# A block inverse in a streaming encoder layer: the first products of its last doubling step get their PSUM bank from a turning pair

## The chip, the core and the metric

The kernel runs on one core of a Trainium2 chip. The metric is the device time of one execution in microseconds (us), lower is better. One execution is also recorded by the hardware profiler; its rows name the engines PE (matrix products), PEld (loading of weights into PE), DVE (vector engine), ACT (scalar engine), POOL (GpSimd) and SP (which issues most transfers).

## What is computed

One layer of an encoder (depth 1) for 512 prompt tokens and 64 sample tokens of width 1024, all in float32. The first half of the layer mixes tokens in two ways from one input projection: four heads of a gated delta rule (GDN), and four heads of differential attention. Then come attention to a memory of 256 tokens and a feed-forward network of width 4096. The change lies in the delta rule, which the reference writes so:

```python
a_sys = jnp.where(strict, bc[..., :, None] * kk * gam, 0.0) + jnp.eye(C)
u = triangular_solve(a_sys, bc[..., None] * vc, lower=True, unit_diagonal=True)
w = triangular_solve(a_sys, (bc * jnp.exp(G))[..., None] * kc, ...)
def step(S, xs):                      # over chunks
    vn = u_c - w_c @ S
    o = qg_c @ S + qk_c @ vn
    S = S * gl_c + kd_c.T @ vn
```

So each chunk of tokens needs a triangular system solved, and the state S passes from chunk to chunk.

## The kernel before, in words

The kernel cuts the 512 prompt tokens into four chunks of 128 (0 to 3) and treats the sample as a fifth (4), with two heads packed into each block. `gdn_prep` (line 653) makes what a chunk needs without the state: normed keys and queries, decay factors, the key products `At`, and the transposed inverse `X` of the unit triangular matrix. The inverse starts from blocks of 2 and doubles: five levels in the loop of line 757 reach blocks of 64. In each level PE turns a block (`bt`) and makes one product (`by`), ACT copies the turned block (line 765), DVE masks the product (766), PE makes the second product (767), and DVE subtracts it (773, 774). A last step from 64 to 128 stands in lines 776 to 788, for chunks 0 to 3 alone: the turned inverse is copied to `X` (line 776), four small products are written to `by` (781) and copied to `Y` (782), and four more give the corner of `X` (785 to 788).

`gdn_scan` (line 814) takes the state through a chunk: it subtracts the state's part from the values (line 830), applies `X` and scales (831 to 833, `vn`), forms the output (840), forms the state's increment in a bank (841) and updates the state `S` on DVE (line 797), and later turns the normed output (850). The sample's scan is cut into steps that lie among the attention heads.

PSUM has eight banks of 512 float32 columns, which line 75 deals out by tag: three to projections (`pr`), two that turn (`ba`), one each to even and odd chunks (`g0`, `g1`), one to the scans (`gs`). `bank(tag)` (line 100) asks for the next bank of a tag; with one bank per tag the next user waits until the last reader is done, with two they take turns. The memory's turned tiles (`turn_memory`, line 905) and the state's increment (line 841) also ask for `ba`. The key tile `kd` of a chunk (line 679) is one of two that take turns between chunks, and it is read last by the chunk's state increment.

The main loop (914 to 924) asks in this order: `gdn_prep` of chunk 0, then for c from 0 to 3 `gdn_prep` of chunk c+1, after c = 0 the memory's turned tiles and the projection `z`, the finish of the scan before, and `gdn_scan` of chunk c. Behind it `diff_project` and `diff_head` (965, 1075) are called for the four attention heads. The program is not run in that order: a scheduler lays out each engine's instructions beforehand, so products of the projections (`pr`, lines 173 to 189) for heads 0 and 1 are laid among the small products of the delta rule. Each engine runs its own row in order.

Of the kernel before, what the change touches and what calls it, by code (L numbers as in the profile page):

```python
# [37 lines left out]
def hybrid_layer_kernel(  # L38
# [40 lines left out]
    def nm(s):  # L79
        uid[0] += 1  # L80
        return f"{s}_{uid[0]}"
# [18 lines left out]
    def bank(tag="ba"):  # L100
        return ps.tile([P, 512], F32, tag=tag, name=nm(tag), bufs=BANKS[tag])
# [4 lines left out]
    def mm(out, lhsT, rhs, start=True, stop=True, pin=False, skip_group_check=False):  # L106
        i = nc.tensor.matmul(out, lhsT, rhs, start=start, stop=stop, skip_group_check=skip_group_check)  # L107
        if pin:
            tc.keep_in_program_order(i)
# [543 lines left out]
    def gdn_prep(c, nb, L):  # L653
# [91 lines left out]
        def pairs(b, half, f):  # L745
            t = b[:, 256 * half : 256 * half + np_ * P].rearrange("p (i n) -> p i n", n=P)
            for i in range(np_):
                f(t[:, i, :], i)
            return t
# [7 lines left out]
        while lv <= last:  # L757
# [6 lines left out]
            by = pairs(b, 0, lambda o, i: mm(o, As[:, i, :], low[:, i * n : (i + 1) * n]))  # L764
# [11 lines left out]
        A.copy(X, each(tr, of(Dt)))  # L776
        if lv < size:
            G.memset(Y[:64, :, :64], 0.0)
            by = bank(f"g{c % 2}")
            for h in range(H):  # L780
                mm(by[64:, h * 64 : h * 64 + 64], At[:, h, 64:], Dt[:, h, :64])
            A.copy(Y[64:, :, :64], by[64:, :256].rearrange("p (h n) -> p h n", h=4))
            bx = bank(f"g{c % 2}")
            for h in range(H):
                mm(bx[:64, h * 64 : h * 64 + 64], Y[:, h, :64], X[:, h, 64:])
            V.tensor_scalar(
                X[:64, :, 64:], bx[:64, :256].rearrange("p (h n) -> p h n", h=4), -1.0, None, ALU.mult
            )
# [124 lines left out]

    S, behind = None, lambda: None
    prepared = [gdn_prep(*chunks[0])]
    for c, _, L in chunks[:4]:
        prepared.append(gdn_prep(*chunks[c + 1]))
        if c == 0:
            turn_memory()
            project_z()  # L920
        behind()
        S, behind = gdn_scan(c, L, prepared[c], S)
        if c == 3:
            behind()
# [792 lines left out]
```

## Time and profile before

| what | value |
|---|---|
| time, median of 3 runs | 977.6 us (976.36 to 977.66) |
| the profiled execution's own time | 977.09 us |
| its span, first to last instruction | 975.3 us |
| PE busy | 960.4 us, 98% of the span, 6399 instructions |
| PEld busy | 889.9 us, 91% |
| DVE busy | 689.4 us, 71% |
| ACT busy | 536.9 us, 55% |
| bytes moved | 96.01 MB, mean 98 GB/s |

The profile's busy time of PE runs from the start of a product to its modelled end; products overlap, so a row of four that starts 0.45 us before the next row can be shown as 0.61 us long. Durations of steps are therefore taken here from start to start. A float32 product of 128x128 stands twice in the trace for each time that the program's order names it (x4 in the order is x8 in the trace); a turn stands once.

### The profile page before, as it was taken

To read this page: it belongs to the slowest core of one execution; us is meant where nothing else is said; L and a number is where in the kernel's file an instruction comes from. 1 tells how busy PE (TensorE), PEld (TensorE's weight loads), DVE (VectorE), ACT (ScalarE), POOL (GpSimd) and SP (SyncE) were. 2 spreads that over 40 slices of the span, in tenths; PEclk is the share of its full clock that TensorE was granted. 3 is DMA by queue.
4 is the path that set the end of the run, shared out by engine and by line. 5 is a ranking of instruction groups with operands and counts; after the bars stand their busy time and mean duration, and the time that the engine had idled before them with its cause. 6 is when DMAs were issued, how large, how long until landed. Compare 5 with 4: busy or idle time off the path is not lost.

```text
span 975.3 us, 16991 instructions
## 1 busy us (share of the span) xinstructions
PE 960.4 (98%) x6399; PEld 889.9 (91%) x6399; DVE 689.4 (71%) x1508; ACT 536.9 (55%) x1218; POOL 66.6 (7%) x158
## 2 busy tenths in 40 slices
PE   9999999998999999999999999999999999999996
PEld 7999998997888878999999999999999999999996
DVE  6655777776867776666657888567867779978674
ACT  6664774533656765435445567665544444545444
POOL 4341020211010000000000000000000000000000
PEclk9999999999999999999999999999999999999999
DMA  7442332120744666341121423332323223322202
GB/s 209 117 138 77 95 125 66 46 64 23 187 122 122 219 182 196 87 130 44 45 65 44 141 69 96 90 88 88 87 81 87 87 87 87 87 87 87 66 23 97
DMA packets 124915, 96.01 MB, mean 98 GB/s; under 512 B 6204, under 2 KB 112846, under 8 KB 124322
## 3 DMA queue, kind: packets, MB, share of 16 engines
q1 hardware_dynamic: 124466, 94.28, 33.6%
q8 instruction: 50, 0.82, 0.4%
q10 hardware_dynamic: 368, 0.66, 0.2%
q14 instruction: 31, 0.25, 0.1%
HBM read 79.93 MB, written 9.75 MB: 92 GB/s over the span
## 4 chain that ended last, share of the span: by engine, by line
PE 58%; issue 2%; DVE 1%; ACT 1%; DMA 0%; POOLq 0%; POOL 0%; ACTq 0%; DVEq 0%; SPq 0%
PE pr L107 37%; PE ba L107 10%; PE g L107 6%; PE gs L107 4%; PE ba L113 1%; DMA raw<-in_w_ff_dram 0%; ACT u L1596 0%; ACT c L1504 0%; DVE u L1552 0%; DVE w2l L1458 0%; ACT c L1503 0%; DVE w L1357 0%; DVE wl L1357 0%; DVE wh L1357 0%; ACT wl L1356 0%
## 5 line engine op out<-in xcount | busy, mean ns | idle before, releaser
L107 PE MATMUL pr<-u,wh 128*128 128x320 f32 (+2 forms) x1240 | 325.9, 341 | 0.1
L107 PE MATMUL pr<-u,wl 128*128 128x256 f32 (+1 forms) x816 | 226.1, 301 | 0.0
L107 PEld LDWEIGHTS pr<-u,wh 128*128 128x128 f32 x1240 | 212.1, 189 | 15.2 <-ACT u L286 0.3
L107 PEld LDWEIGHTS pr<-u,wl 128*128 128x128 f32 x816 | 150.5, 189 | 2.5 <-DVE wl L387 0.2
L160 DVE TENSOR_TENSOR wl<-raw,wh 128x1024 fp32r<-128x1024 f32 x65 | 79.5, 1223 | 56.5 <-ACT wh L159 56.3
L159 ACT CAST wh<-raw 128x1024 fp32r<-128x1024 f32 x65 | 68.2, 1049 | 61.9 <-PE pr L107 46.6
L107 PE MATMUL pr<-u,w2h 128*128 128x320 f32 (+1 forms) x384 | 98.5, 341 | 0.0
L1457 ACT CAST w2h<-r 128x512 fp32r<-128x512 f32 x56 | 34.7, 620 | 87.6 <-PE pr L107 85.4
L107 PE MATMUL pr<-f,w2h 128*128 128x320 f32 (+1 forms) x288 | 74.5, 341 | 0.5 <-DVE u L1546 0.5
L107 PEld LDWEIGHTS pr<-u,w2h 128*128 128x128 f32 x384 | 65.0, 188 | 4.5 <-ACT u L1542 0.3
L107 PE MATMUL pr<-u,w2l 128*128 128x256 f32 (+1 forms) x256 | 65.2, 296 | 0.0
L1544 DVE TENSOR_TENSOR u<-u,pr 128x256 f32<-128x256 f32 x96 | 42.4, 450 | 17.1 <-PE pr L107 16.5
L206 POOL TENSOR_TENSOR tiny<-tiny,nhalf 128x1 f32<-128x1 f32 (+4 forms) x10 | 8.8, 879 | 651.3 <-DVE tiny L1610 514.1
L107 PE MATMUL ba<-u,wl 128*128 128x288 f32 x360 | 52.9, 296 | 0.0
L107 PEld LDWEIGHTS pr<-f,w2h 128*128 128x128 f32 x288 | 48.8, 188 | 4.5 <-issue 1.7
L107 PEld LDWEIGHTS ba<-u,wl 128*128 128x128 f32 x360 | 49.2, 188 | 0.6 <-ACT keep L1494 0.5
L107 PE MATMUL pr<-f,w2l 128*128 128x256 f32 (+1 forms) x192 | 48.9, 295 | 0.0
L107 PEld LDWEIGHTS pr<-u,w2l 128*128 128x128 f32 x256 | 47.0, 189 | 1.5
L1458 DVE TENSOR_TENSOR w2l<-r,w2h 128x512 fp32r<-128x512 f32 x56 | 38.5, 688 | 9.6 <-ACT w2h L1457 9.4
L107 PE MATMUL pr<-wh,u 128*128 128x512 f32 x128 | 41.6, 400 | 0.1
L1503 ACT ACTIVATE c<-c 128x288 f32<-128x288 f32 x48 | 20.6, 443 | 28.5 <-DVE c L1502 28.5
L107 PEld LDWEIGHTS pr<-f,w2l 128*128 128x128 f32 x192 | 35.2, 189 | 1.1
(552 smaller groups left out, 2024.8 us busy)
## 6 DMA issues: line engine op xcount, KB each, us to landing
raw<-in_w_ff_dram SPq DMA_DIRECT2D x36, 512.0 KB
raw<-in_w_in_dram SPq DMA_DIRECT2D x28, 512.0 KB
r<-in_w_ff_dram SPq DMA_DIRECT2D x56, 256.0 KB
raw<-in_w_mem_k_dram SPq DMA_DIRECT2D x8, 512.0 KB
raw<-in_w_mem_v_dram SPq DMA_DIRECT2D x8, 512.0 KB
raw<-in_w_out_dram SPq DMA_DIRECT2D x8, 512.0 KB
raw<-in_w_mem_q_dram SPq DMA_DIRECT2D x8, 512.0 KB
raw<-in_w_mem_o_dram SPq DMA_DIRECT2D x8, 512.0 KB
```

What stands on the lines that cost most here:

```text
L107: i = nc.tensor.matmul(out, lhsT, rhs, start=start, stop=stop, skip_group_check=skip_group_check)
L113: i = nc.tensor.transpose(out, in_, ident[:n, :n])
L159: A.copy(wh, raw)
L160: V.tensor_tensor(wl, raw, wh.bitcast(F32), ALU.subtract)
L206: G.tensor_tensor(out, in_, bc(nhalf[: in_.shape[0], 0:1], list(in_.shape)), ALU.pow)
L1457: A.copy(wh, src)
L1458: V.tensor_tensor(wl, src, wh.bitcast(F32), ALU.subtract)
L1503: A.activation(c, c, AF.Relu)
L1544: V.tensor_tensor(am, am, b, ALU.add)
```

## The change

One word of line 779 goes: the bank of the small products `by` in the step from blocks of 64 to 128 is asked for with the default tag `ba` in place of the chunk's own `g0` or `g1`.

```diff
         A.copy(X, each(tr, of(Dt)))
         if lv < size:
             G.memset(Y[:64, :, :64], 0.0)
-            by = bank(f"g{c % 2}")
+            by = bank()
             for h in range(H):
                 mm(by[64:, h * 64 : h * 64 + 64], At[:, h, 64:], Dt[:, h, :64])
```

The arithmetic is the same, and each engine has the same work. What moves is the order that the scheduler makes. In the names below `g0_…` and `g1_…` are banks of even and odd chunks, `ba_…` the turning pair, `gs_…` the scans' bank, `pr_…` the projections'. The numbers behind a name count the tiles.

On PE, before, the increment of the state by chunk 1 (`ba_319`) stood directly behind the output of that scan (`gs_318`), while the inverse of chunk 2 was in its second level (`g0_300`):

```order
L107 MATMUL gs_318_2092<-S_267_1889,u_4_78 128x128
L107 MATMUL gs_318_2092<-vn_317_2090,KQ_207_1500 128x128
L107 MATMUL ba_319_2101<-vn_317_2090,kd_196_1456 128x128 x3
L107 MATMUL g0_300_2003<-Y0_291_1967,X_290_1966 128x128 x2
L107 MATMUL ba_319_2101<-vn_317_2090,kd_196_1456 128x128
L107 MATMUL pr_527_3020<-u_6_91,wh_525_3016 128x512
```

Now it stands behind the last step of that inverse (`ba_311` are its small products), near the end of the last projection of heads 0 and 1 (`pr_539`):

```order
L113 MATMUL g0_310_2052<-ident_79,Dt0_292_1968 128x128 x4
L107 MATMUL ba_311_2059<-Dt0_292_1968,At0_283_1941 64x64 x4
L107 MATMUL ba_319_2101<-vn_317_2090,kd_196_1456 128x128 x4
L107 MATMUL g0_312_2065<-X_290_1966,Y0_291_1967 64x64 x4
L107 MATMUL pr_539_3120<-u_7_92,wh_534_3092 128x320
```

The increment moved from the second level of chunk 2's inverse to behind its small products, which the program asks for earlier from the same pair. The increment by chunk 2 (`ba_370`) stands behind chunk 3's small products (`ba_362`) in the same way.

On DVE, before, the update of the state (line 797) and behind it the first work of chunk 3 (`kd_326`, line 680) stood in the second level of chunk 2's inverse:

```order
L773 TENSOR_TENSOR Y0_291_1967<-Dt0_292_1968,g0_300_2003 128x32x4
L797 SCALAR_TENSOR_TENSOR S_267_1889<-S_267_1889,egl_1227,ba_319_2101 128x128
L774 TENSOR_TENSOR Dt0_292_1968<-Dt0_292_1968,g0_300_2003 128x64x4
L797 SCALAR_TENSOR_TENSOR S_267_1889<-S_267_1889,egl_1227,ba_319_2101 128x128 x3
L680 TENSOR_TENSOR kd_326_2126<-g1_325_2121,kdc_1228 128x512
```

Now they stand behind the fifth level's subtraction (`g0_309`) and the corner of `X` (line 786), and a split of weights for a later projection (`wl_609`) comes next:

```order
L774 TENSOR_TENSOR Dt0_292_1968<-Dt0_292_1968,g0_309_2048 128x8x32
L797 SCALAR_TENSOR_TENSOR S_267_1889<-S_267_1889,egl_1227,ba_319_2101 128x128 x2
L786 TENSOR_SCALAR X_290_1966<-g0_312_2065 64x4x64
L797 SCALAR_TENSOR_TENSOR S_267_1889<-S_267_1889,egl_1227,ba_319_2101 128x128 x2
L680 TENSOR_TENSOR kd_326_2126<-g1_325_2121,kdc_1228 128x512
L160 TENSOR_TENSOR wl_609_3420<-raw_607_3417,wh_608_3419 128x1024
```

So chunk 3's preparation begins behind chunk 2's whole inverse.

On PE, before, the last products of `pr_539` stood among the end of chunk 3's inverse: its fifth level (`g1_360`), the turn of line 776 (`g1_361`) and its small products (`g1_362`), and the opening of chunk 4 (`g0_391`, `g0_397`):

```order
L107 MATMUL pr_539_3120<-u_7_92,wl_535_3093 128x320 x2
L107 MATMUL pr_539_3120<-u_7_92,wh_534_3092 128x320
L107 MATMUL g1_360_2265<-Y1_342_2184,X_341_2183 128x128 x2
L113 MATMUL g0_391_2381<-ident_79,u_1_75 128x128 x2
L107 MATMUL pr_539_3120<-u_7_92,wh_534_3092 128x320
L113 MATMUL g1_361_2269<-ident_79,Dt1_343_2185 128x128 x4
L113 MATMUL g0_397_2395<-ident_79,X_393_2389 128x128 x2
L107 MATMUL g1_362_2276<-Dt1_343_2185,At1_335_2160 64x64 x4
```

Now they stand ahead of the products that open chunk 3 (`g1_328`, `g1_334`, `g1_336`, the queries and the key products), and up to the turned output of the third scan (`gs_424`) no projection follows:

```order
L107 MATMUL pr_539_3120<-u_7_92,wh_534_3092 128x320 x2
L113 MATMUL g1_328_2131<-ident_79,u_4_78 128x128 x4
L107 MATMUL g1_334_2155<-u_1_75 128x128 x4
L113 MATMUL gs_364_2289<-ident_79,on_320_2110 128x128 x4
L107 MATMUL g1_336_2165<-u_4_78,u_1_75 128x128 x4
L107 MATMUL gs_365_2295<-S_267_1889,u_1_75 128x128 x4
L113 MATMUL g1_339_2173<-ident_79,u_1_75 128x128 x4
L113 MATMUL g1_345_2189<-ident_79,X_341_2183 128x128 x4
L107 MATMUL gs_367_2302<-on_366_2300,X_290_1966 128x128 x4
L113 MATMUL g1_347_2198<-ident_79,Y1_342_2184 128x128 x2
```

In both programs the next projection (`pr_605`, head 2) stands directly behind the last product of `gs_424`. The memory's turned tiles, which also use the pair, moved from before the inverses of chunks 0 and 1 to behind them; projections stand on both sides of them in both programs. From within the projection of the memory's values on, PE's order is the same.

## The prediction

> **What bounds the kernel now.** The page comes first:
>
> ```profile
> span 975.3 us, 16991 instructions
> PE 960.4 (98%) x6399; PEld 889.9 (91%) x6399; DVE 689.4 (71%) x1508; ACT 536.9 (55%) x1218; POOL 66.6 (7%) x158
> ```
>
> PE is busy for 98% of the span, so whatever leaves PE without a ready product is time lost, and work on other engines costs only where PE waits for it. The profiled execution took 977.09 us, 1.8 us more than its span, and lies 0.5 us below the median of the three runs; I work against it. Then the waits of PE and the stretch table around the delta rule's end:
>
> ```profile
> PE gs L107 <- DVE vn L833: 0.8, 1, 0.8
> PE g L107 <- ACT X L776: 0.6, 1, 0.6
> 214.00:232.00 18.00, 17.96 (x140) 16.58 (x138) 12.77 (x37) 5.88 (x19) 3.26 (x8) 1.00 0.11 30
> 232.00:246.00 14.00, 11.42 (x92) 9.41 (x90) 8.54 (x24) 7.77 (x25) 1.92 (x5) 1.00 0.23 58
> ```
>
> Single waits are 0.8 us and less. From 214 to 232 us PE is covered: projections of heads 0 and 1 lie among the small products of chunk 3. From 232 to 246 it is bare: PE idles 2.6 us by the shown ends. The timeline of PE shows both ends of the bare stretch:
>
> ```profile
> 230.49 0.39 PE L107 MATMUL pr<-u,wh 128*128 128x320 f32 x1
> 230.72 0.46 PE L107 MATMUL pr<-u,wl 128*128 128x320 f32 x2
> 231.02 0.30 PE L107 MATMUL pr<-u,wh 128*128 128x320 f32 x1
> 231.26 0.71 PE L107 MATMUL g<-Y,X 128*128 128x128 f32 x4
> ...
> 231.95 0.39 PE L107 MATMUL pr<-u,wh 128*128 128x320 f32 x1
> 232.49 0.66 PE L113 MATMUL g<-ident,Dt 128*128 128x128 f32 x4
> ...
> 233.96 0.68 PE L107 MATMUL g<-Dt,At 128*64 128x64 f32 x8 [0.60 <-ACT X L776]
> 235.19 0.65 PE L107 MATMUL g<-X,Y 128*64 128x64 f32 x8 [0.55 <-ACT Y L782]
> ...
> 236.34 0.94 PE L107 MATMUL gs<-on,X 128*128 128x128 f32 x6
> ...
> 245.96 0.48 PE L107 MATMUL pr<-u,wh 128*128 128x512 f32 x1
> ```
>
> The last projection of heads 0 and 1 ends at 232.1; chunk 3's small products, the ones the change is about, start at 233.96, the corner at 235.19, the third scan's `X` product at 236.34; the next projection (head 2) starts at 245.96. So chunk 3's inverse is all but finished when the cover runs out. The price of the bare stretch before is 13.9 us, of which PE works most.
>
> **What the change does, part by part.**
>
> *The work itself* costs nothing: the same 16 small products with the same evacuations. *The bank* frees one wait: `by` no longer stands behind the copy of line 776 (0.60 us in the row at 233.96). Of four chunks only chunk 3's shows such a wait; the others have projections in it.
>
> *The order* is the cost. The pair `ba` is dealt out as the program asks, and `gdn_prep` of chunk c+1 asks ahead of `gdn_scan` of chunk c. So the state's increment by chunk 1 now stands on PE behind chunk 2's small products, the state's update and chunk 3's `kd` stand behind it on DVE, and chunk 3's preparation starts when chunk 2's inverse ends, where before the two overlapped. The projections that would cover chunk 3 have by then been spent on chunk 2; between the last `pr_539` and `pr_605` PE has only the chain.
>
> *When the cover ends now.* Up to the last `pr_539` the new order leaves out what the old one had done by then for chunk 3, the second scan and the opening of chunk 4: by the two orders, 150 passes of 128x128 (turns once, products twice; the five levels are 10 each). Their pace, and what a level takes:
>
> ```profile
> 189.96 1.05 PE L107 MATMUL gs<-on,X 128*128 128x128 f32 x8
> 190.87 0.71 PE L107 MATMUL g<-Y,X 128*128 128x128 f32 x4
> ...
> 211.94 0.66 PE L113 MATMUL g<-ident,X 128*128 128x128 f32 x4
> ...
> 214.37 0.38 PE L113 MATMUL g<-ident,Y 128*128 128x128 f32 x2
> ...
> 216.15 0.68 PE L107 MATMUL g<-Y,X 128*128 128x128 f32 x4
> ...
> 217.78 0.39 PE L113 MATMUL g<-ident,Y 128*128 128x128 f32 x2
> ...
> 219.59 0.71 PE L107 MATMUL g<-Y,X 128*128 128x128 f32 x4
> ...
> 241.54 0.30 PE L113 MATMUL g<-ident,Y 128*128 128x128 f32 x1
> ...
> 242.86 0.49 PE L107 MATMUL g<-Y,X 128*128 128x128 f32 x2
> ...
> 244.21 0.30 PE L113 MATMUL g<-ident,Y 128*128 128x128 f32 x1
> ```
>
> Eight passes take 0.91 us (189.96 to 190.87), so 150 take 16.5 to 17 us. Each return to a projection costs 0.23 us for its first product (230.49 to 230.72) against 0.15 for the next ones: 0.08 more, some twenty times, 1.7 us. The last projection thus ends near 232.1 − 16.6 − 1.7 = 213.8 us, with PE full until then.
>
> *Chunk 3's front, from the state's increment to the turn of X.* Behind the increment PE has 8 products of 0.15 us, 8 small passes and 2 turns before the projection ends, 1.9 us, so the increment ends near 211.9. DVE then does the following, by these rows:
>
> ```profile
> 197.36 0.68 DVE L680 TENSOR_TENSOR kd<-g,kdc 128x512 f32<-128x512 f32 x1
> ...
> 206.53 0.69 DVE L736 SCALAR_TENSOR_TENSOR B<-lev,At 128x512 f32<-128x512 f32 x1
> 207.13 0.69 DVE L716 TENSOR_TENSOR KQ<-g,Y 128x512 f32<-128x512 f32 x1
> ...
> 212.46 1.21 DVE L160 TENSOR_TENSOR wl<-raw,wh 128x1024 fp32r<-128x1024 f32 x1
> ...
> 219.45 0.86 DVE L797 SCALAR_TENSOR_TENSOR S<-S,egl,ba 128x128 f32<-128x128 f32 x3
> ...
> 221.13 0.42 DVE L680 TENSOR_TENSOR kd<-g,kdc 128x256 f32<-128x256 f32 x1
> ...
> 225.76 0.74 DVE L851 SCALAR_TENSOR_TENSOR u<-gs,gcol,u 128x512 f32<-128x512 f32 x1
> ```
>
> and ACT casts the weights that DVE's line 160 splits:
>
> ```profile
> 211.20 1.04 ACT L159 CAST wh<-raw 128x1024 fp32r<-128x1024 f32 x1 [0.27 <-PE pr L107]
> ```
>
> State update and corner 1.5 us, so `kd` starts near 213.4 and ends at 214.0 (one 128x512 operation costs 0.60, from 206.53 to 207.13). Then comes the weight split, whose cast on ACT can only start when the last `pr_539` has freed the tile: 213.8 + 1.04 + 1.21 = 216.2. Behind it three 128x512 operations and small ones, 2.1 (218.3); the four rows of `At` at 0.27 each, 1.1 (219.4); line 851, 0.7 (220.1); six 128x512 operations, 3.6 (223.7); the handover to PE, an estimate of 0.5. `X` is turned near 224.2, against 211.94 before: **+12.3 us**.
>
> *The levels.* Before, from 211.94 to the corner at 235.19, 23.25 us with projections in between. Bare, a level's first half is 1.8 us (217.78 to 219.59) whatever lies beside it, as this is a chain of PE, ACT and DVE. Its second half is between 1.35 (chunk 4, half as wide, 242.86 to 244.21) and 1.63 (216.15 to 217.78); I take 1.45, since chunk 4's is bare as this will be. Four levels and a half: 4 × 3.25 + 1.8 = 14.8. The opening is 1.6 (2.43 before, with a weight split of 1.21 on DVE in it), the end 1.23 (231.26 to 232.49) + 0.4 + 1.23 (233.96 to 235.19, without the 0.60), and the second scan's DVE steps among them 0.7. Sum 20.0: the corner comes near 244.2, and **−3.3 us** are gained on the levels.
>
> *From the corner to the next projection.* Before, the third scan's `X` product came 1.15 us behind the corner (236.34), as DVE had made its right side before the corner. Now the state's update by chunk 2, chunk 4's `kd`, reductions, decay factors and `At` stand ahead of it on DVE, 4.8 us of the rows above at half width (0.42 shown), with 0.9 of handovers to ACT and PE; with the corner's own 1.1, the rest of the state's update 0.5 and line 830 with handover 0.75 it comes 8.05 behind the corner: **+6.9 us**. The rest (9.6 us from 236.34 to 245.96) stays, less 0.4 for a level of chunk 4 that now falls behind.
>
> Sum: 12.3 − 3.3 + 6.9 − 0.4 = 15.5 us; the next projection starts at 261.5. In a bare stretch of 47.7 us PE has at most 28 us of work (the 16.6 and the 11.4 shown from 232 to 246). Later little can be given back; in the table of 25 us stretches PE idles 0.1, 0.6 and 0.8 us in these:
>
> ```profile
> 250.00:275.00 25.00, 24.93 (x163) 22.06 (x162) 19.98 (x69) 15.47 (x55) 0.16 (x1) 1.00 0.67 166
> 275.00:300.00 25.00, 24.37 (x158) 21.85 (x156) 16.27 (x52) 14.52 (x48) 2.61 (x6) 1.00 0.42 117
> ...
> 350.00:375.00 25.00, 24.19 (x120) 19.60 (x119) 17.47 (x21) 15.60 (x25) 1.36 (x2) 1.00 0.58 171
> ```
>
> I give 0.5 back: +15, so 977.1 + 15 = **992.1 us**. Low bound: DVE's front without the weight split's wait (−2), levels at chunk 4's 2.67 us (−2.6) and the second front half hidden (−3), which gives +7.4: 985. High bound: the front at its old pace (197.36 to 211.94, 14.6 us: +4), the levels at theirs (+3.3), chunk 4's front a third longer (+2.5): +25, 1002.
>
> **The rivals.**
>
> *Faster: the freed bank counts and the order does not.* If chunk 3 were still covered, only the 0.60 at 233.96 would go, at best 0.60 more where `Y` is copied early: 976 us. It decides at one point: `gs_424` must end by 245.9, so the bare chain would have to fit into 32 us where the sum has 47.7. The Trainium skill speaks for this rival ("PSUM — Partial Sum Buffer", section "PSUM bank collisions raise a hardware error"): two engines must not be on one bank and quadrant at once, so a product into another bank may run beside the copy. This trace agrees that the copy held the product (0.60). Chance 3%.
>
> *PE's clock falls in the bare stretch.* The record shows when it does:
>
> ```profile
> 965.00:970.00 5.00, 2.43 (x22) 2.19 (x22) 2.49 (x6) 2.42 (x5) 0.85 (x1) 1.00 0.04 14
> 970.00:975.00 5.00, 0.00 (x0) 0.00 (x0) 0.40 (x1) 0.57 (x1) 0.00 (x0) 0.56 0.78 248
> ```
>
> With PE half busy the granted clock was still 1.00, and so it was from 232 to 246; without any product it fell within 5 us. In the bare chain PE works a little over half the time, and the longest gaps of the sum are some 2 us. If it fell all the same, PE's 11 us on the chain (1.1 in each of five levels, the rest in both fronts and the scan) would double: 992 + 10 = 1002. The Trainium skill ("TensorE: Matmul & The Clock Gate", Part 1) puts the fall at an idle window of about 3.4 us; no gap of the sum reaches that. Chance 10%.
>
> *The chain is faster or partly covered:* DVE and ACT alone in the bare stretch, as in the low bound, 985 to 988: 15%. *The chain keeps its old pace,* as in the high bound, 997 to 1002: 15%. The forecast, 988 to 997, has the other 57%.
>
> The range 985 to 1002 takes in the bounds of the chain and leaves out the faster rival and what lies beyond those bounds. About 0.2% (2 us) is what a measurement of this kernel can tell from no change. Faster has 3%, same 1%, slower 96%.
>
> **What would show it.** In the changed kernel's timeline, the last projection of head 1 should end near 214 and the next start near 261, with PE working little more than half of the time between; chunk 3's first turn of `X` near 224, its corner near 244, each level at 3.2 to 3.4 us. The small products should follow the turn of line 776 without a wait for ACT. The granted clock should stay 1.00. I am wrong if a projection lies between them, if the scan of chunk 1 updates the state early, or if the gap is given back after 262: then the span's growth would be less than that of the bare stretch.

## The result and the profile after

| what | before | after |
|---|---|---|
| time, median of 4 runs each | 977.63 us (976.36 to 977.70) | 1004.84 us (1004.60 to 1004.95) |
| ratio to before, 95% interval | | 1.0279 [1.0264, 1.0293] |
| the profiled execution: time, span | 977.09, 975.3 us | 1004.8, 1003.0 us |
| its mean granted clock | 0.998 | 0.984 |

One execution each of two of the experiments (both with the state's increment in the chunk's own bank) took 1875 and 2563 us; such slow runs are left out of every ratio and interval here.

Slower, as forecast, but by 27.2 us where the forecast had 14.5 (992.1 against 977.6), and beyond the end of its range, 1002. The page of the changed kernel, span and busy times:

```profile
span 1003.0 us, 17000 instructions
PE 973.7 (97%) x6399; PEld 898.6 (90%) x6399; DVE 692.7 (69%) x1508; ACT 539.0 (54%) x1218; POOL 66.4 (7%) x158
```

The span grew by 27.7 us, and PE's part of that has two halves: idle time went from 14.9 to 29.3 us (+14.4), and busy time from 960.4 to 973.7 (+13.3) with the same 6399 instructions. The first half is lost cover. The second means that products ran longer or, no longer overlapped by others, are shown longer. The waits of PE (us in total, times, longest):

```profile
PE g L107 <- DVE Y L766: 3.9, 4, 1.0
PE g L113 <- ACT B L682: 3.6, 2, 1.8
```

The first row is the levels of an inverse, one behind the other, each wait 1 us and less; the second is the opening of a chunk's preparation. The longest single wait of the stretch is 1.85 us, at 254.90 in chunk 4's opening. The two stretches that the prediction compared, busy time of PE, PEld, DVE, ACT and POOL, then the granted clock:

```profile
214.00:232.00 18.00, 12.47 (x84) 10.97 (x83) 12.63 (x26) 5.66 (x11) 2.62 (x4) 0.91 0.16 45
232.00:246.00 14.00, 7.43 (x34) 5.76 (x32) 4.46 (x11) 3.01 (x10) 1.62 (x4) 0.65 0.00 0
```

In place of 17.96 and 11.42 us PE works 12.47 and 7.43, and part of that at a lower clock. PE's timeline from the last projection of heads 0 and 1 to the next:

```profile
214.20 0.53 PE L107 MATMUL pr<-u,wh 128*128 128x320 f32 x2
...
225.30 0.63 PE L113 MATMUL g<-ident,X 128*128 128x128 f32 x4 [1.83 <-DVE X L737]
...
231.53 0.41 PE L113 MATMUL g<-ident,Y 128*128 128x128 f32 x2
...
235.00 0.41 PE L113 MATMUL g<-ident,Y 128*128 128x128 f32 x2 [0.93 <-DVE Dt L774]
235.25 0.61 PE L107 MATMUL g<-Dt,B 128*128 128x128 f32 x4
...
238.98 0.66 PE L113 MATMUL g<-ident,Y 128*128 128x128 f32 x2 [0.93 <-DVE Dt L774]
239.43 1.06 PE L107 MATMUL g<-Dt,B 128*128 128x128 f32 x4
...
243.61 0.66 PE L113 MATMUL g<-ident,Y 128*128 128x128 f32 x2 [0.93 <-DVE Dt L774]
...
247.83 1.12 PE L113 MATMUL g<-ident,Dt 128*128 128x128 f32 x4 [0.52 <-DVE Dt L774]
248.88 1.12 PE L107 MATMUL ba<-Dt,At 128*64 128x64 f32 x8
...
251.94 1.12 PE L107 MATMUL g<-X,Y 128*64 128x64 f32 x8
...
262.00 1.23 PE L107 MATMUL gs<-on,X 128*128 128x128 f32 x4
...
272.62 0.50 PE L107 MATMUL pr<-u,wh 128*128 128x512 f32 x1
```

No projection lies between 214.7 and 272.62; chunk 3's whole inverse is bare, as forecast. The small products (248.88) follow the turn (247.83) with no wait for ACT, as forecast. But a level takes 3.47 us from 231.53 to 235.00, and 4.63 from 238.98 to 243.61: its first products take 1.06 us (239.43) where those at 235.25 take 0.61, while the wait ahead of the turn is 0.93 both times. The same stretch in slices of 3.41 us, cut where the clock's record steps, shows why:

```profile
215.85:219.26 3.41, 1.93 (x13) 1.50 (x14) 3.23 (x6) 1.74 (x3) 0.01 (x1) 1.00 0.22 51
...
222.68:226.09 3.41, 1.57 (x13) 1.17 (x12) 3.07 (x6) 0.95 (x3) 0.00 (x0) 1.00 0.00 0
226.09:229.50 3.41, 3.41 (x18) 3.41 (x18) 1.25 (x3) 1.30 (x4) 0.00 (x0) 0.50 0.00 0
...
232.92:236.33 3.41, 1.57 (x10) 1.22 (x10) 1.09 (x3) 0.92 (x4) 1.62 (x4) 1.00 0.00 0
236.33:239.74 3.41, 1.99 (x8) 1.72 (x9) 1.13 (x3) 0.31 (x2) 0.00 (x0) 0.50 0.00 0
...
253.40:256.81 3.41, 1.15 (x6) 0.72 (x6) 2.47 (x9) 0.77 (x2) 0.00 (x0) 1.00 0.00 0
256.81:260.22 3.41, 3.05 (x13) 2.65 (x14) 2.78 (x11) 0.69 (x2) 1.63 (x4) 0.50 0.03 5
```

PE's clock stood at one half for 27.3 us in all between 226 and 264. It fell three times, each time behind a slice in which PE worked 1.57 us or less, and it stayed behind one of 1.93. In the eight slices at one half PE is shown busy for 21.8 us, so the half clock accounts for at most half of that, 10.9 us, of the 13.3 by which PE's busy time grew; the rest was not split by any run.

### The profile page after: what moved, and what is told of

Same layout as the page of the kernel before. It is cut to its first block, busy times and chain, and to the rows that moved or that the text cites. A ratio compares the mean times of both kernels' runs of the same rounds, so it can differ in the third digit from the quotient of the medians.

```text
span 1003.0 us, 17000 instructions
## 1 busy us (share of the span) xinstructions
PE 973.7 (97%) x6399; PEld 898.6 (90%) x6399; DVE 692.7 (69%) x1508; ACT 539.0 (54%) x1218; POOL 66.4 (7%) x158
## 4 chain that ended last, share of the span: by engine, by line
PE 91%; DVE 3%; ACT 2%; issue 2%; POOL 0%; POOLq 0%; ACTq 0%; DVEq 0%
PE pr L107 55%; PE g L107 12%; PE ba L107 12%; PE gs L107 7%; PE ba L113 3%; PE g L113 2%; DVE p L459 0%; ACT wh L159 0%; PE pr L113 0%; DVE Dt L774 0%; ACT u L1596 0%; DVE Y L766 0%; ACT u L221 0%; DVE tg L687 0%; ACT aT L1110 0%
```

## The experiments

All times are compared with runs of the kernel before on the same chip (977.3 to 977.6 us). "Bare passes" are the 128x128 passes that the order of PE has between the last projection of heads 0 and 1 and the next projection: 80 before the change, 225 after.

**What costs: the bank, or its turn?** The first kernel keeps the small products in the pair and moves the whole last step of each inverse behind the scan of the chunk before, so that the state's increment uses the pair first.

```diff
+        def corner():
             G.memset(Y[:64, :, :64], 0.0)
             by = bank()
...
         S, behind = gdn_scan(c, L, prepared[c], S)
+        if c < 3:
+            prepared[c + 1]["corner"]()
```

> The last step of each inverse (its four small products into the turning pair, the copy, the corner) stands in the program behind the scan of the chunk before, so that the state's increment asks the pair first; the small products stay in the pair. Theory A (the turn of asking in the pair is what costs): the increments stand early on PE again, 81 passes of 128x128 lie between the last projection of heads 0 and 1 and the next one (80 before the change, 225 after), the clock stays 1.00, and the time is 976.5 to 978 us. Rival B (small products in the pair are slow in themselves, or the pair is too full with them): 1000 us or more, as after the change.

Measured 977.96 us, ratio 1.0003 [0.9994, 1.0012]. PE's timeline at the end of chunk 3's inverse:

```profile
232.82 0.66 PE L113 MATMUL g<-ident,Dt 128*128 128x128 f32 x4 [0.29 <-DVE Dt L774]
233.41 0.68 PE L107 MATMUL ba<-Dt,At 128*64 128x64 f32 x8
...
245.62 0.50 PE L107 MATMUL pr<-u,wh 128*128 128x512 f32 x1
```

The whole loss is gone with the small products still in the pair, so it is the turn that costs, not the bank. The freed wait is seen too: the small products follow the turn after 0.59 us where it was 1.47 before. Of that the next projection kept 0.34 us (245.62 for 245.96), which the time cannot show.

**Which chunk?** Three kernels that use the pair for some chunks only. Chunk 2 alone:

```diff
-            by = bank()
+            by = bank("ba" if c == 2 else f"g{c % 2}")
```

> Only chunk 2's small products go into the pair, the other chunks' stay in their own bank. Theory A: only the increment by chunk 1 is late, so chunk 3's preparation starts about 13 us later (turn of its X near 225), while chunk 4's preparation overlaps chunk 3's levels; of the 26.7 us that the next projection came later, the front's 13.4 and the levels' 3.4 stay, and the 8.9 behind the corner go, for 986 us with the clock at 1.00 and up to 996 with it at one half for a part. Rival C (the memory's turned tiles, which the change moves behind the inverses of chunks 0 and 1, carry the cost): 977.6, as they stay where they were here.

Measured 990.96 us, ratio 1.0138 [1.0125, 1.0152]. The turn of chunk 3's `X`, the corner, the third scan's `X` product and the next projection:

```profile
224.83 1.06 PE L113 MATMUL g<-ident,X 128*128 128x128 f32 x4
...
248.12 0.65 PE L107 MATMUL g<-X,Y 128*64 128x64 f32 x8
...
249.28 0.94 PE L107 MATMUL gs<-on,X 128*128 128x128 f32 x6
...
258.73 0.50 PE L107 MATMUL pr<-u,wh 128*128 128x512 f32 x1
```

`X` is turned at 224.83, 12.9 us later than before, and from there to the end the stretch is as before: 23.3 us to the corner, 1.16 to the scan. So this kernel has the late front of chunk 3 and nothing else but one slice of 3.41 us at the half clock; the time lies inside what was expected. Chunk 3 alone:

```diff
-            by = bank()
+            by = bank("ba" if c == 3 else f"g{c % 2}")
```

> Only chunk 3's small products go into the pair. Theory A: the increment by chunk 1 is early and chunk 3's inverse is covered by projections; only the increment by chunk 2 is late, so chunk 4's preparation starts behind chunk 3's corner: +7 to +9 us, 984.5 to 987, the sum of this and of chunk 2's part near the whole +27. Rival C (the memory's turned tiles carry the cost): 977.6. Rival B (small products in the pair are slow): under 979, as one step of four uses the pair.

Measured 987.42 us, ratio 1.0106 [1.0092, 1.0119]. The same places:

```profile
235.91 0.97 PE L107 MATMUL g<-X,Y 128*64 128x64 f32 x8
...
245.83 1.17 PE L107 MATMUL gs<-on,X 128*128 128x128 f32 x4
```

The corner comes where it was before (235.19), but the third scan's product 9.9 us behind it in place of 1.15: chunk 4's front stands between them. The time is 0.4 above what was expected; the clock was at one half here too, for 13.7 us, and the 9.9 us contain what that cost. Chunks 0 and 1 alone, which also moves the memory's turned tiles:

```diff
-            by = bank()
+            by = bank("ba" if c < 2 else f"g{c % 2}")
```

> Only the small products of chunks 0 and 1 go into the pair, so the memory's turned tiles move behind the inverses of chunks 0 and 1 as in the changed kernel, and the increments by chunks 1 and 2 stay early. Theory A and the prediction's line that this move costs nothing: 977 to 980 us, though 145 passes now lie between the last projection of heads 0 and 1 and the next. Rival C (the memory's tiles carry the cost): 990 us or more.

Measured 981.45 us, ratio 1.0043 [1.0029, 1.0056], 1.5 above the expectation. Neither the theory's range nor the rival's holds it. The clock stayed at 1.00, and PE is idle for 5.9 us of these 25, where before it was 2.6 (nearly all of it in the bare stretch from 232 to 246):

```profile
225.00:250.00 25.00, 19.11 (x148) 16.00 (x146) 17.75 (x52) 11.49 (x36) 3.56 (x9) 1.00 0.23 60
```

So even with both late increments undone the new order spends projections earlier (the last of heads 0 and 1 starts at 224.1, before at 231.95), and the new order costs 4.1 us. What part of this the moved tiles of the memory have, no run shows. The three parts make 13.4 + 9.9 + 4.1 = 27.4 us, against 27.2 for the whole change; that they add up so closely is not shown to be more than a coincidence, since the clock fell for different times in each.

**Through what does the late increment act?** In the next kernel the increments stay late, but chunk 3's `kd` has a tile of its own (that of a later stage, free until then), so that it need not wait for the increment by chunk 1:

```diff
-        kd = sb("kd")[:, :nb]
+        kd = (cp.tile([P, 4, P], F32, tag="vs", name=nm("kd")) if c == 3 else sb("kd"))[:, :nb]
```

> The changed kernel in which chunk 3's kd has a tile of its own, so that its preparation need not wait for the increment by chunk 1; the increments stay late. Theory A (the late increment hurts because kd waits for it): chunk 3's preparation starts early again, its levels lie under the projections, 115 passes lie bare, and only the part behind chunk 3's corner stays: 982 to 988 us. Rival E (the late state alone holds the scan back, kd does not matter): 995 us or more.

Measured 979.67 us, ratio 1.0023 [1.0014, 1.0032], better than expected. PE's timeline:

```profile
209.79 0.60 PE L113 MATMUL g<-ident,X 128*128 128x128 f32 x4
...
215.04 1.16 PE L107 MATMUL ba<-vn,kd 128*128 128x128 f32 x8
...
225.13 0.70 PE L107 MATMUL g<-triu,gg 128*128 128x128 f32 x4
...
232.16 1.16 PE L107 MATMUL ba<-vn,kd 128*128 128x128 f32 x8
```

The increment by chunk 1 (215.04) is as late as ever, but chunk 3's `X` is turned at 209.79, ahead of it. Chunk 4's opening (225.13) is early too, ahead of the increment by chunk 2 (232.16), which the expectation had not seen: with one chunk less in the pair of `kd` tiles, chunk 4's waits for the increment by chunk 1 and not for that by chunk 2. So 25 of the 27 us pass through the two tiles of `kd`, and rival E, the late state alone, is out. In the last kernel of this group the increment leaves the pair, the small products stay in it:

```diff
-        b = each(lambda o, h: mm(o, q["kd"][:, h, :], vn[:, h, :]), "ba")
+        b = each(lambda o, h: mm(o, q["kd"][:, h, :], vn[:, h, :]), f"g{c % 2}")
```

> The changed kernel, small products in the pair, but the state's increment in the chunk's own bank. Theory A: the increment no longer stands behind the small products, chunk 3's preparation starts early, 126 passes lie bare, of which the chain of chunk 3 is only the end: 978 to 985 us. Rival B (small products in the pair cost by themselves): 1000 or more.

Measured 979.94 us, ratio 1.0027 [1.0015, 1.0040]: once the two no longer share the pair, 25 us are gone. Rival B is out by this run and the first.

**What part has the clock?** Three kernels put products that nobody reads into PE's gaps, by a bank of the pair that chunks 3 and 4 hold for this. They add work and leave the chain's order nearly as it is. The first has 150 passes by its page (6549 instructions of PE where the others have 6399), two more than the expectation says:

```diff
+        w = bank() if c in (3, 4) else None
+        def fill(n, x, y, m=2):
+            if w is not None:
+                for i in range(n):
+                    mm(w[:, i % 4 * P : i % 4 * P + P], x[:, i % m, :], y[:, i % m, :])
...
+            fill(4 if c == 3 else 0, As, Ds)
             A.copy(Xs, bt)
...
+            fill(3 if c == 3 else 0, Xs, Yc)
```

> The changed kernel with 148 passes of products that nobody reads (17 us of work) put into a bank of the pair, spread over the preparation of chunks 3 and 4 and the levels of chunk 3 so that they fill PE's gaps; the order of the rest is kept. Theory A with the clock (lost overlap costs 15 us, the half clock the other 11): the granted clock stays 1.00, the levels of chunk 3 take 3.3 to 3.6 us each, and the time falls to 991 to 997 us although PE does more. Rival D (the levels are slow by their chain alone, the clock only follows): the levels keep their 4.2 to 4.6 us, the filling comes on top, 1005 to 1020.

Measured 1003.87 us, ratio 1.0267 [1.0253, 1.0281]. The clock did stay at 1.00 through the levels, and they took 3.50 us each:

```profile
232.50 0.38 PE L113 MATMUL g<-ident,Y 128*128 128x128 f32 x2
...
236.00 0.38 PE L113 MATMUL g<-ident,Y 128*128 128x128 f32 x2
...
248.77 0.68 PE L107 MATMUL g<-X,Y 128*64 128x64 f32 x8
250.97 1.13 PE L107 MATMUL ba<-kd 128*128 128x128 f32 x8 [1.52 <-DVE kd L687]
```

The corner came 3.2 us earlier, but this was given back: behind it filling stood ahead of chunk 4's first products (250.97), and the clock fell there all the same. The time lies between the two expectations, so as a test of it the run is inconclusive. With 106 passes by its page (6505 instructions; the expectation says 104), in smaller portions and some around the last step; this diff is against the first filled kernel:

```diff
-            fill(4 if c == 3 else 0, As, Ds)
+            fill(2 if c == 3 else 0, As, Ds)
...
-            fill(3 if c == 3 else 0, Xs, Yc)
+            fill(2 if c == 3 else 0, Xs, Yc)
...
+            fill(4 if c == 3 else 0, Dt, Dt)
             by = bank()
```

> As in the filled kernel, but with 104 passes of filling (12 us) in smaller portions, also around the last step of chunk 3, so that no step of the chain waits behind a portion. Theory A with the clock: the granted clock stays 1.00 until the next projection, chunk 3's X is turned before 226.5, a level takes 3.5 us, the corner comes before 248.5 and the next projection before 268; 994 to 999 us, so the half clock costs 6 to 10 us. Rival D (the chain is slow by itself, the clock only follows): 1004 us or more.

Measured 1002.90 us, ratio 1.0261 [1.0246, 1.0277]. Corner at 248.04, and again a portion stood behind it and the clock fell at 253.6; the time lies between the expectations again. The two traces showed where PE had room, and the third filling, 64 passes, keeps to that: none ahead of the turn of `X` or of the small products, none in the two levels with scan products, six products on chunk 3's finished `X` at the head of chunk 4's preparation (this diff is against the changed kernel):

```diff
+        if c == 4:
+            fill(6, prepared[3]["X"], prepared[3]["X"])
...
+            fill(2 if c == 3 and lv >= 8 else 0, As, Ds)
```

> Filling again, 64 passes (7 us), placed by the two filled kernels' traces only where PE idled: nothing ahead of the turn of X, nothing in the two levels that have scan products, nothing between the turn of line 776 and the small products, and six products at the head of chunk 4's preparation. Theory A with the clock: clock 1.00 up to the next projection, levels of 3.47 us, the corner near 245.5, the next projection near 264, 995 to 998 us: the half clock costs 7 to 10 us. Rival F (the levels gain 4 us from the clock, but chunk 4's front does not): the corner near 246, the next projection near 269, 1000 to 1002 us, so the half clock costs 3 to 5 us and the rest of the missing 12 is in the chain.

Measured 1000.15 us, ratio 1.0234 [1.0217, 1.0251], with 7 us more of products than after the change and 4.7 us less time. The timeline (its lines of code are numbered some 13 higher here):

```profile
225.50 0.63 PE L113 MATMUL g<-ident,X 128*128 128x128 f32 x4 [0.94 <-DVE X L749]
...
234.18 0.41 PE L113 MATMUL g<-ident,Y 128*128 128x128 f32 x2
...
237.65 0.41 PE L113 MATMUL g<-ident,Y 128*128 128x128 f32 x2
...
246.78 0.68 PE L107 MATMUL g<-X,Y 128*64 128x64 f32 x8
...
256.10 0.71 PE L107 MATMUL gs<-on,X 128*128 128x128 f32 x4
...
266.71 0.50 PE L107 MATMUL pr<-u,wh 128*128 128x512 f32 x1
```

And its slices where the clock fell:

```profile
214.21:217.62 3.41, 1.77 (x12) 1.08 (x10) 2.28 (x3) 2.20 (x4) 0.00 (x0) 1.00 0.00 0
217.62:221.04 3.42, 3.33 (x15) 3.33 (x16) 2.92 (x10) 0.59 (x2) 1.83 (x2) 0.50 0.86 228
```

The clock was at one half for a single slice, early in the front, and a level took 3.47 us. Rival D is out: a level takes 3.47 us at the full clock and 4.63 at one half. The times fit rival F's 1000 to 1002, the timeline lies between the two: the next projection comes 5.9 us earlier than after the change, of which 4.7 reach the time. So the clock has about 5 to 6 of the 12.7 us by which the profiled run after lies above the forecast, and the rest is in the chain itself. Filling may still have delayed something, so the clock's part may be a little more.

**A version faster than both.** The kernel before, with the increment in the chunk's own bank and the small products there too:

```diff
             by = bank(f"g{c % 2}")
...
-        b = each(lambda o, h: mm(o, q["kd"][:, h, :], vn[:, h, :]), "ba")
+        b = each(lambda o, h: mm(o, q["kd"][:, h, :], vn[:, h, :]), f"g{c % 2}")
```

> The kernel before with one other word changed: the state's increment goes into the chunk's own bank and no longer into the pair, and the small products stay in the chunk's own bank too. The order then has head 2's first projection directly behind the last of head 1, ahead of chunk 3's last step, so the bare stretch of the kernel before (232 to 246 us, 2.6 us of idle PE) has products of a projection in it: 974.5 to 976.5 us, faster than both kernels. If the stretch was not what PE lost, 977.6.

Measured 975.53 us, ratio to before 0.9983 [0.9974, 0.9992]. The stretch that was bare before:

```profile
232.00:246.00 14.00, 13.97 (x111) 12.54 (x109) 9.02 (x25) 7.13 (x21) 1.72 (x4) 1.00 0.16 39
```

And PE's timeline, the first product of head 2's projection:

```profile
233.59 0.47 PE L107 MATMUL pr<-u,wh 128*128 128x512 f32 x1
```

Head 2's projection starts at 233.59 in place of 245.96, while chunk 3's inverse is in its end, and PE idles 0.03 us of the 14 in place of 2.6. The time fell by 1.8 us: a small gain, but outside the interval, and 29 us below the changed kernel.

## Why the prediction was right and wrong

The direction and its mechanism were right, and the runs show each link: the turn in the pair puts the increment behind the small products (removed by the late last step, and by the increment in the chunk's own bank), the late increment holds back `kd` and with it the next chunk's preparation (removed by `kd`'s own tile), and the projections are spent before (none from 214.7 to 272.62). The rival "the freed bank counts and the order does not" is out: with the order mended, the freed wait gave nothing that can be measured.

The size was wrong. Step by step, with the least filled kernel as what the chain takes at the full clock (its own front aside, where one slice was at one half):

| step | forecast | after | least filled |
|---|---|---|---|
| last projection of heads 0 and 1 ends | 213.8 | 214.7 | 214.6 |
| chunk 3's `X` turned | 224.2 | 225.30 | 225.50 |
| from there to the corner | 20.0 | 26.64 | 21.28 |
| corner to the third scan's `X` product | 8.05 | 10.06 | 9.32 |
| from there to the next projection | 9.2 | 10.62 | 10.61 |
| next projection starts | 261.5 | 272.62 | 266.71 |

*The step that failed* is the rival of the clock, which got 10% and whose price was not in the sum. The prediction argued that the clock would stay at 1.00, since it was so with PE half busy in a 5 us stretch of the kernel before and since no gap reached 3.4 us. No gap did (the longest is 1.85 us), and the clock fell three times. The 5 us row was a bad witness. The slice of the kernel before that holds most of it, its length and then PE's busy time first:

```profile
967.18:970.60 3.42, 0.25 (x3) 0.01 (x1) 2.23 (x4) 1.95 (x3) 0.85 (x1) 1.00 0.24 86
```

In the slice ahead of it (963.77 to 967.18) PE was busy all through. So the "half busy" stretch was the end of a full slice and most of a nearly empty one, and behind that one the clock fell. From 232 to 246, the other witness, PE was busy for 82%. And "a little over half the time" was an average over the bare stretch: the prediction's own figure for a level, 1.1 us of PE's work in 3.25, is a third, and the slice from 232.92, which covers about one level, had 1.57 of 3.41. Every step of the record between two changes of the clock is a multiple of 3.413 us. The rule of the Trainium skill that the prediction leant on ("TensorE: Matmul & The Clock Gate", Part 1: the clock falls after an idle window of about 3.4 us) has that length right, but here the window was not idle: half busy was enough to lose the clock. The section "A second HAM failure mode: psum-queue depth-cycling" of that page of the Trainium skill tells of short idles between groups of products that make the clock swing. That fits what this chain does, and the prediction should have set it against Part 1.

Measured against the least filled kernel, the clock takes 5.4 us up to the corner and 0.7 of chunk 4's front: 6.1, not the 10 that the rival's price had. That price took the clock to be low in the whole bare stretch; it was low for 27.3 of its 57.9 us. (Half of the increment by chunk 2 stands ahead of the corner in the least filled kernel and all of it after the change, which shifts about 0.6 us between the two parts and leaves their sum.)

*Terms that were mis-sized.* Four of them, each by 1.1 to 1.4 us, all to the same side and, but for the clock's part above, at the full clock: chunk 3's front with the end of the cover (1.1; the weight split on DVE, set down to end at 216.2 though its own sum gives 216.05, ended at 217.07), the levels (21.28 for 20.0: a level is 3.47 and not 3.25, as its second half was taken at 1.45, near chunk 4's 1.35, and is about 1.65, 3.47 less the first half's 1.81: the 1.63 that stood at 216.15 was the right row), chunk 4's front (9.32 for 8.05), and the way to the next projection (10.6, not 9.2; nothing of it went away). Together 5.1. Behind the next projection the span grew by another 1.0 us where 0.5 were to be given back, 1.5 more; no run shows what made these. 6.1 + 5.1 + 1.5 = 12.7, all of the 12.7 us between 992.1 and the profiled 1004.8.

*The range.* Its upper end, 1002, took the chain slow at the full clock or the clock low with the chain as forecast, never both. Either alone would have stayed inside: 992.1 + 6.1 is 998, and 992.1 + 5.1 + 1.5 is 999. The two share their condition, a bare chain, and came together, but the prediction priced such rivals one at a time.

*A cost that was not listed.* The order around chunks 0 and 1 was described and given no price; by itself it costs 4.1 us.

## What to carry to other kernels

A buffer that two users take in turn also orders the two users: before moving a write into such a pool, list who uses it next in program order, and what waits for that one, as a freed wait of 0.6 us here bought a delay of 13. When a stretch loses its filler work, take PE's share of each 3.4 us and not of the whole stretch; where it is about half or less, as in the slices behind which the clock fell here, price the chain at the lower clock, together with the longer chain. And to take a user out of a shared pool can pay: the increment in the chunk's own bank gave the only version that was faster.

## What the runs showed of the hardware

The granted clock goes by fixed slices of 3.413 us and by how much PE worked in the slice, not by the longest gap. Between 210 and 285 us it fell nine times in six of the kernels, each time behind a slice with 0.98 to 1.77 us of PE work (29 to 52%); behind slices with 1.93 us and more (57%) it stayed at 1.00, in these kernels and in the kernel before, whose lowest slice there has 2.25. The line between the two is not sharp: at the end of the span, where the last products run out, the clock also fell behind slices with 1.86 us (the changed kernel with the increment in the chunk's own bank), 1.97 (chunk 3 alone in the pair) and 2.00 (chunks 0 and 1 alone). The slice with the least work behind which it fell, in the kernel with chunk 2 alone in the pair (the slice behind it, at one half, is in the last table below):

```profile
219.66:223.08 3.42, 0.98 (x7) 0.56 (x6) 3.42 (x7) 0.42 (x1) 0.07 (x1) 1.00 0.58 153
```

To come back takes more than to stay: at one half, slices with 1.97 to 3.05 us of work left the clock low (3.05 in the row at 256.81 above), others with 2.90 to 3.41 brought it back. Turns count less there. The products alone (line 107, without the turns of line 113) of three slices of the changed kernel, of which the first and the third left it low and the second brought it back, and of the slice of chunk 2's kernel above, which brought it back:

```profile
246.57:249.98 3.41, 1.85 (x13) 1.44 (x12) 0.50 0.00 0
249.98:253.40 3.42, 3.07 (x17) 2.66 (x16) 0.50 0.00 0
256.81:260.22 3.41, 1.93 (x9) 1.93 (x10) 0.50 0.03 5
223.08:226.49 3.41, 2.25 (x8) 1.90 (x8) 0.50 0.00 0
```

With the turns they have 2.89, 3.07, 3.05 and 2.90 us, which does not tell them apart; the products alone do. This holds for all eighteen slices at one half between 210 and 285 us in the six kernels: nine with 1.52 to 1.98 us of products left the clock low, nine with 2.25 and more brought it back. "TensorE: Matmul & The Clock Gate" in the Trainium skill (Part 4) says that a turn does not count as busy in the same way, which fits this. The falls do not ask for it: with products alone a slice of 1.16 stayed and one of 1.32 fell. No run here was made to settle how turns count.
